# A dense SwiGLU layer with seven of eight quarter products in both halves, and expert tiles of other row counts

## The chip, the cores and the metric

The kernel runs on one core of one Trainium2 chip. The metric is the device time of one execution in microseconds. The kernel before was timed three times: median 3994.94 us, lowest 3988.59, highest 4003.63.

## The reference, cut to what matters

A trunk of two residual layers over 1024 tokens of width 1024, all in float32. The even layer ends in a dense SwiGLU with 2816 inner columns, the odd one in a mixture of eight experts with 3584 inner columns, of which each token takes two:

```python
h = h + retnet_gla_mixer(hn, positions, ...)          # ends in  o @ w_out
h = h + swiglu(rms_norm(h, norm_ffn_g[0]), w_gate, w_up, w_down)
h = h + hgrn2_mixer(hn, ...)
h = h + moe_swiglu(rms_norm(h, norm_ffn_g[1]), w_router, w_gate, w_up, w_down)
return rms_norm(h, final_norm_g)

def swiglu(h, w_gate, w_up, w_down):
    return (jax.nn.silu(h @ w_gate) * (h @ w_up)) @ w_down

def moe_swiglu(h, w_router, w_gate, w_up, w_down):
    top_logits, top_idx = lax.top_k(xt @ w_router, 2)
    ...
```

## The kernel before, in words

**Products.** Every float32 matrix is held as a high and a low part (`whi`, `wlo`; `xhi`, `xlo`), and a block product is three TensorE matmuls, high by high, high by low and low by high (`mm3`, L153). The parts are made on two engines: ScalarE copies the high part, VectorE subtracts it to get the low one (`split_to`, L819; `split`, L136). A block has 128 stationary columns; the moving side has 512 columns in the dense layer and as many as the expert tile has rows in the experts. PSUM has two rings of four banks, `pj` and `dn`.

**Order of the work.** The program is traced in order, and a list scheduler then fixes each engine's own order; an engine runs its list strictly from the front. All loads go through SyncE's queue (SP), the stores through GpSimd's (POOL). Work that may come later is handed to `defer` (L102), which runs it some ticks on; a tick is one step of the loop under way.

**Projection, L750 to L790.** Eight token tiles of 128 rows; each is 48 matmuls of 512 columns, then the residual add (L766). One tick later `done` stores the row tile, takes its norm (L188) and `place` turns it: eight TensorE transposes into PSUM, evacuated as high and low parts (L198). The halves `x[0]`, `x[1]` of turned rows are the input of the dense layer.

**Dense layer, first product, L813 to L932.** Tokens and input columns are cut in two, so the input has four quarters; gate and up columns stand as the two halves of the other side. Seven products of sums of quarters replace the eight quarter products. `quad_sums` (L823) makes the three sums from the already turned halves: add high and low (L836), combine (L841), split again (L820, L821). `quad_weights` (L866) does the like for the weights of each of 22 column blocks; each block then runs seven products of 12 matmuls, and stores its hidden tile of 128 x 1024 to scratch.

**Dense layer, second product, `ffn_down`, L934 to L980.** A plain product: token tiles in groups of 3, 3 and 2 (L42), for each group 22 inner blocks, for each block 2 column halves by each tile by 3 matmuls of 512. Each group reads the hidden rows from scratch and the whole of `ffn_w_down`. Ahead of the first hidden tile the queue carries the gain of the next norm and three row tiles `h` (L935 to L955).

**Experts, L1237 to L1388.** Eight stages in an order of load: the first is the expert with the fewest picks among the first 768 tokens, the others follow by falling count. Stage n computes a tile of `CAPS[n]` rows (L31). Gate and up are 1344 matmuls with `CAPS[n]` moving columns. Down has two forms (L1324): up to two cuts of 128 rows it is 336 matmuls of 512 columns; with three cuts of 96 it is 672 matmuls of `CAPS[n]` columns and transposes back. When an expert has more picks than its stage's rows, a branch after the eight stages runs a further whole tile of 288 rows for it and adds up all rows anew (L1258, L1481).

Of the kernel before, what the change touches and what calls it, by code (L numbers as in the profile page):

```python
# [9 lines left out]
F32 = mybir.dt.float32  # L10
F32R = mybir.dt.float32r
# [19 lines left out]
CAPS = (256, 288, 284, 280, 272, 264, 256, 256)  # L31
# [10 lines left out]
FFN_TILES = ((0, 3), (3, 3), (6, 2))  # L42
# [33 lines left out]
class Trunk:  # L76
# [136 lines left out]
    def gain_rows(self, pool, tag, ap):  # L213
        g = self.t(pool, [P, D], tag)
        self.nc.sync.dma_start(g, self.bcast_rows(ap, D))
        return g


    def build(self, upto=9):
        nc, tc = self.nc, self.tc  # L220
        with ExitStack() as ctx:
# [8 lines left out]
            with self.pool("hnp") as self.hnp:  # L230
# [3 lines left out]
                with self.pool("op") as self.op, self.pool("w2") as w2:  # L234
                    x = self.outproj_ab(oT, (w2, 0, 4))
                if upto < 2:
                    return
                pc = self.ffn(x)
# [511 lines left out]
    def outproj(self, w, src, oT, w2, pairs, done):  # L750
# [8 lines left out]
        for t in range(8):  # L759
            h = self.t(self.op, [P, D], "h", 6)  # L760
# [11 lines left out]
    def outproj_ab(self, oT, w2):  # L772

        nc = self.nc
        g = self.gain_rows(self.op, "gain", self.i["norm_ffn_g"][0])
        x = [None, None]

        def place(hn, t):
            if t % 4 == 0:
                x[t // 4] = self.half()  # L780
            self.rows_to_fm(self.dn, hn, x[t // 4], t % 4)

        def done(h, t):
            nc.gpsimd.dma_start(self.s["h0"][t * P:(t + 1) * P, :], h)
            hn = self.norm_rows(self.op, "hn", h, g)

            self.defer(max(1, 4 * (t // 4) + 3 - t), place, hn, t)

        self.outproj(self.i["ab_w_out"][0], self.i["x"][0], oT, w2, (0, 2, 3, 1), done)
        self.flush()  # L790
        return x
# [21 lines left out]
    def ffn(self, x):  # L813

        with self.pool("ffs") as fs:
            self.gate_up_quads(fs, x)
        return self.ffn_down(x)

    def split_to(self, hi, lo, src):  # L819
        self.nc.scalar.activation(hi, src, AF.Copy)  # L820
        self.nc.vector.tensor_tensor(lo, src, hi.bitcast(F32), op=OP.subtract)  # L821

    def quad_sums(self, fs, x):  # L823


        tt = self.nc.vector.tensor_tensor
        quarter = [[[a[:, 4 * c:4 * c + 4, :] for a in x[r]] for c in range(2)] for r in range(2)]

        def tiles():
            return [self.t(fs, [P, 2, HT], "raw", 8) for _ in range(2)]  # L830

        def whole(q):
            out = tiles()
            for n, o in enumerate(out):
                hi, lo = (a[:, 2 * n:2 * n + 2, :].bitcast(F32) for a in q)
                tt(o, hi, lo, op=OP.add)  # L836
            return out

        def sums(dst, a, b, op):
            for o, p, q in zip(dst, a, b):  # L840
                tt(o, p, q, op=op)  # L841
            return dst

        def split(src, name):
            s = [self.t(fs, [P, 4, HT], name + n, 1, F32R) for n in ("hi", "lo")]
            for n, r in enumerate(src):
                self.split_to(*(a[:, 2 * n:2 * n + 2, :] for a in s), r)
            return s

        a21, a22 = whole(quarter[1][0]), whole(quarter[1][1])  # L850
        s1 = sums(a22, a21, a22, OP.add)
        o1 = split(s1, "s1")
        a11 = whole(quarter[0][0])
        s2 = sums(s1, s1, a11, OP.subtract)
        o2 = split(s2, "s2")
        s3 = sums(a21, a11, a21, OP.subtract)
        a12 = whole(quarter[0][1])
        s4 = sums(a12, a12, s2, OP.subtract)

        o4 = quarter[1][0]  # L860
        for n, r in enumerate(s4):
            self.split_to(*(a[:, 2 * n:2 * n + 2, :] for a in o4), r)
        o3 = split(s3, "s3")
        return [quarter[0][0], quarter[0][1], o4, quarter[1][1], o1, o2, o3]

    def quad_weights(self, fs, w, v, c):  # L866

        nc = self.nc
        g, u = (self.t(fs, [P, 2, 4, P], "raw", 8) for _ in range(2))
# [3 lines left out]
        ta, tb = (self.t(fs, [P, 2, 4, P], "raw", 8) for _ in range(2))  # L873
        tt, wp = nc.vector.tensor_tensor, self.wps[0][0]
# [23 lines left out]
    def gate_up_quads(self, fs, x):  # L898
# [3 lines left out]
        wg, wu = (i[k][0] for k in ("ffn_w_gate", "ffn_w_up"))  # L902
        tt, act = nc.vector.tensor_tensor, nc.scalar.activation
        X = None
        for f in range(D_FF // P):
            W = self.quad_weights(fs, wg, wu, f * P)
            X = X or self.quad_sums(fs, x)
            A, B = self.pj([P, HT]), self.dn([P, HT])
            C, Dk = self.pj([P, HT]), self.dn([P, HT])
            p1, d, p5, u2 = (self.t(fs, [P, HT], "sn", 8) for _ in range(4))  # L910
            self.quad_product(A, W[0], X[0], True)
            act(p1, A, AF.Copy)
            self.quad_product(B, W[1], X[1], True)
            tt(p1, p1, B, op=OP.add)
# [19 lines left out]
    def ffn_down(self, x):  # L934
# [4 lines left out]
        with self.pool("ffn") as fp:  # L939
# [8 lines left out]
            for t0, nt in FFN_TILES:  # L948
# [21 lines left out]
                if t0 + nt == 8:  # L970
                    pc = self.piece(i["c_w_in"][0], 2048)
# [604 lines left out]
```

## Time and profile before

| what | value |
|---|---|
| median of three runs | 3994.94 us |
| the profiled execution's own time | 4001.33 us |
| its span, first to last instruction | 3999.7 us |
| TensorE busy | 3890.8 us, 97% of the span |
| VectorE, ScalarE, GpSimd busy | 51%, 38%, 7% |
| mean granted TensorE clock | 0.985 of full |

A row of stretches reads: the stretch in us from the span's start, its length, then busy us and count of instructions of PE (TensorE matmul), PEld (weight load), DVE (VectorE), ACT (ScalarE) and POOL (GpSimd), the granted clock, the share of the DMA engines, GB/s. A row of groups reads: line, engine, operation, output from input, shapes, count, busy us, mean ns of one, idle time before them and what ended it. A row of the timeline reads: start, length (from the first start to the last end of a merged run), engine, line, what, count, and in brackets the idle time before it. Matmuls are pipelined, so the length of one says less than the distance between starts.

### The profile page before, as it was taken

The page shows a single profiled execution, that of the slowest core. Times are in us where ns is not written, and L with a number is a line of the kernel's source. Part 1 is how long each engine was busy: PE and PEld are TensorE (multiplying, and loading weights), DVE is VectorE, ACT ScalarE, POOL GpSimd, SP SyncE. Part 2 cuts the span into 40 slices and gives each one's busy share as a digit, 9 for nine tenths or more (in the row PEclk, how much of TensorE's full clock was granted, in tenths as well). Part 3 has the DMA queues.
Part 4 walks back from the last instruction along what each step waited for, and adds up shares of the span by engine and source line. Part 5 has one row for each costly group of instructions (what it writes and reads, how often), then busy time and mean ns, then how long its engine had stood idle before and what let it go on. Part 6 is the DMA issues. An engine that isn't in the chain of part 4 may idle for free. (4 is left out here: it accounts for less than half of the span.)

```text
span 3999.7 us, 63991 instructions
## 1 busy us (share of the span) xinstructions
PE 3890.8 (97%) x26112; PEld 3600.7 (90%) x26112; DVE 2042.7 (51%) x3011; ACT 1500.2 (38%) x2311; POOL 279.9 (7%) x421
## 2 busy tenths in 40 slices
PE   8999989999899999999899999999999999999998
PEld 7888868888688889997798999999999999999996
DVE  5743356554355364354654544545545445455564
ACT  4212323333334222222344444434434444444443
POOL 1011000000001000003100000000000000000012
PEclk9999989999999999999899999999999999999999
DMA  4011313221665111113566555555555555556686
GB/s 133 27 48 61 127 51 99 82 82 64 193 199 184 43 33 53 43 64 123 169 194 196 168 172 172 171 161 187 185 174 177 179 185 186 189 186 199 216 285 220
DMA packets 436287, 568.17 MB, mean 142 GB/s; under 512 B 25462, under 2 KB 340118, under 8 KB 435984
## 3 DMA queue, kind: packets, MB, share of 16 engines
q1 hardware_dynamic: 414848, 493.87, 38.7%
q0 software_dynamic: 21136, 70.13, 5.0%
q8 instruction: 206, 3.38, 0.4%
q14 instruction: 97, 0.79, 0.1%
HBM read 511.11 MB, written 51.87 MB: 141 GB/s over the span
## 5 line engine op out<-in xcount | busy, mean ns | idle before, releaser
L144 DVE TENSOR_TENSOR wlo<-wst,whi 128x1024 fp32r<-128x1024 f32 (+1 forms) x816 | 995.8, 1223 | 1279.5 <-ACT whi L143 1263.8
L143 ACT ACTIVATE whi<-wst 128x1024 fp32r<-128x1024 f32 (+1 forms) x816 | 859.5, 1056 | 1092.1 <-PE pj L156 583.9
L156 PE MATMUL pj<-mxl,whi 128*128 128x256 f32 (+5 forms) x3584 | 1029.1, 287 | 0.0
L155 PE MATMUL pj<-mxh,whi 128*128 128x256 f32 (+5 forms) x3584 | 1027.6, 287 | 1.0 <-ACT sl L1316 0.6
L157 PE MATMUL pj<-mxh,wlo 128*128 128x256 f32 (+5 forms) x3584 | 1028.5, 287 | 0.0
L155 PEld LDWEIGHTS pj<-mxh,whi 128*128 128x128 f32 x3584 | 675.9, 189 | 1.8 <-ACT sl L1316 0.8
L156 PEld LDWEIGHTS pj<-mxl,whi 128*128 128x128 f32 x3584 | 675.6, 189 | 0.3 <-DVE mxl L1299 0.2
L157 PEld LDWEIGHTS pj<-mxh,wlo 128*128 128x128 f32 x3584 | 673.7, 188 | 0.0
L155 PE MATMUL pj<-whi,xhi 128*128 128x256 f32 (+2 forms) x1280 | 400.8, 314 | 5.0 <-DVE h L976 4.0
L156 PE MATMUL pj<-wlo,xhi 128*128 128x256 f32 (+2 forms) x1280 | 399.2, 312 | 0.9 <-DVE wlo L144 0.9
L157 PE MATMUL pj<-whi,xlo 128*128 128x256 f32 (+2 forms) x1280 | 399.1, 312 | 0.0
L155 PE MATMUL dn<-mhh,whi 128*128 128x288 f32 (+4 forms) x1120 | 326.3, 291 | 0.0
L157 PE MATMUL dn<-mhh,wlo 128*128 128x288 f32 (+4 forms) x1120 | 325.6, 291 | 0.0
L156 PE MATMUL dn<-mhl,whi 128*128 128x288 f32 (+4 forms) x1120 | 325.2, 290 | 0.0
L155 PEld LDWEIGHTS pj<-whi,xhi 128*128 128x128 f32 x1280 | 248.8, 195 | 17.9 <-issue 4.7
L156 PEld LDWEIGHTS pj<-wlo,xhi 128*128 128x128 f32 x1280 | 249.0, 195 | 11.5 <-DVE wlo L144 2.1
L157 PEld LDWEIGHTS pj<-whi,xlo 128*128 128x128 f32 x1280 | 248.7, 194 | 9.1
L155 PE MATMUL pj<-xhi,whi 128*128 128x512 f32 x624 | 246.1, 394 | 5.3 <-ACT whi L820 3.4
L157 PE MATMUL pj<-xhi,wlo 128*128 128x512 f32 x624 | 245.4, 393 | 0.1
L156 PE MATMUL pj<-xlo,whi 128*128 128x512 f32 x624 | 244.8, 392 | 0.0
L156 PEld LDWEIGHTS dn<-mhl,whi 128*128 128x128 f32 x1120 | 210.9, 188 | 0.0
L155 PEld LDWEIGHTS dn<-mhh,whi 128*128 128x128 f32 x1120 | 210.6, 188 | 0.0
(373 smaller groups left out, 5459.7 us busy)
## 6 DMA issues: line engine op xcount, KB each, us to landing
wst<-in_moe_w_gate_dram SPq DMA_DIRECT2D x224, 512.0 KB
wst<-in_moe_w_up_dram SPq DMA_DIRECT2D x224, 512.0 KB
wst<-in_moe_w_down_dram SPq DMA_DIRECT2D x224, 512.0 KB
wst<-in_ffn_w_down_dram SPq DMA_DIRECT2D x66, 512.0 KB
wst<-in_c_w_in_dram SPq DMA_DIRECT2D x32, 512.0 KB
wst<-in_ab_w_in_dram SPq DMA_DIRECT2D x26, 512.0 KB
scr_h<-h POOLq DMA_DIRECT2D x24, 512.0 KB, 3.5
raw<-in_ffn_w_gate_dram SPq DMA_DIRECT2D x22, 512.0 KB
```

Source lines behind the costliest of these rows:

```text
L143: act = nc.scalar.activation(hi, st, AF.Copy)
L144: dve = nc.vector.tensor_tensor(lo, st, hi.bitcast(F32), op=OP.subtract)
L155: mm(ps, l[0], r[0], start=start, stop=False, **kw)
L156: mm(ps, l[0], r[1], start=False, stop=False, **kw)
L157: self.last_mm = mm(ps, l[1], r[0], start=False, stop=stop, **kw)
```

## The change

`CAPS` becomes (224, 284, 280, 276, 270, 256, 248, 256). `quad_sums` goes; the sums of quarters are made from row tiles while the projection runs, in `done`, and turned. The second product is also done as seven products of sums of quarters, each 11 inner blocks by 4 token tiles by 3 matmuls of 512. For this the first product takes its column blocks in pairs (j and j + 11), makes the hidden sums on VectorE and the weight sums of `ffn_w_down` on GpSimd, and stores both to scratch with `keep`, eleven stores to a pair. `ffn_down` reads one stored left and one right block pair (512 KB each) per step; the rows `h` and the gain are loaded at the third tick.

```diff
-CAPS = (256, 288, 284, 280, 272, 264, 256, 256)
+CAPS = (224, 284, 280, 276, 270, 256, 248, 256)
...
+    def turn(self, rows, dst, t):
+        ps = self.dn([P, 4, P])
+        for k in range(4):
+            self.nc.tensor.transpose(ps[:, k, :], rows[:, k * P:(k + 1) * P], self.ident)
+        self.split_to(*(a[:, :, t * P:(t + 1) * P] for a in dst), ps)
...
+        def place2(hn, t, ht, s1):
+            self.turn(hn[:, R], q[1][1], t)
+            self.turn(s1, X[0], t)
+            self.turn(ht[:, L], X[1], t)
+            self.turn(ht[:, R], q[1][0], t)
         def done(h, t):
             nc.gpsimd.dma_start(self.s["h0"][t * P:(t + 1) * P, :], h)
             hn = self.norm_rows(self.op, "hn", h, g)
+            if t < 4:
+                nc.gpsimd.dma_start(self.s["hn0"][t * P:(t + 1) * P, :], hn)
+                self.defer(1, place, hn, t)
+                return
+            ht = self.t(self.op, [P, D], "ht", 1)
+            r = slice((t - 4) * P, (t - 3) * P)
+            nc.sync.dma_start(ht, self.s["hn0"][r, :])
+            s1 = h[:, L]
+            tt = (nc.vector if t > 5 else nc.gpsimd).tensor_tensor
+            tt(s1, hn[:, L], hn[:, R], op=OP.add)
+            tt(hn[:, L], ht[:, L], hn[:, L], op=OP.subtract)
+            tt(ht[:, L], s1, ht[:, L], op=OP.subtract)
+            tt(ht[:, R], ht[:, R], ht[:, L], op=OP.subtract)
+            nc.gpsimd.dma_start(self.s["s3r"][r, :], hn[:, L])
+            self.defer(1, place2, hn, t - 4, ht, s1)
+        self.outproj(self.i["ab_w_out"][0], self.i["x"][0], oT, w2, (0, 2, 3, 1), done, 3)
...
+            sn = lambda: self.t(fs, [P, HT], "sn", 10)
+            for f in [a * NH + j for j in range(NH) for a in range(2)]:
...
+                if f == 0:
+                    for t in range(4):
+                        r = sn()
+                        nc.sync.dma_start(r, self.s["s3r"][t * P:(t + 1) * P, :])
+                        self.turn(r, X[6], t)
...
+                if f < NH:
+                    a11, a21 = p1, d
+                    b = self.t(fs, [P, 2, 2, HT], "wd", 1)
+                    nc.sync.dma_start(b, wd.rearrange("(r p) (c n) -> p r c n", p=P, c=2)[:, j::NH])
+                else:
+                    a12, a22 = p1, d
...
+                    tt(s1, a21, a22, op=OP.add)
+                    self.keep("hid", 4, j, s1)
...
+                    tt(a11, s1, a11, op=OP.subtract)
+                    self.keep("hid", 5, j, a11)
...
+                    pt(b[:, 0, 0], b[:, 0, 1], b[:, 0, 0], op=OP.subtract)
...
+                    for n, a in enumerate((b[:, 0, 0], b[:, 1, 1], b[:, 0, 1], b[:, 1, 0])):
+                        self.keep("wt", n, j, a)
...
     def ffn_down(self, x):
+            def product(n, ps, first=True, last=True):
+                for j0 in range(0, NH, 2):
...
+                    own = n or j0 > 2
+                    for dst, src, pool in ((l, hv[n], fp if own else None), (r, W[n], None)):
+                        wp = self.wps[0][0]
+                        st = self.t(pool or wp, [P, 2, HT], "wst", 4 if pool else 2)[:, :nj]
+                        nc.sync.dma_start(st, src[:, js])
+                        dst += [self.t(pool or wp, [P, 2, HT], a, 3 if pool else 4, F32R)[:, :nj] for a in ("whi", "wlo")]
+                        self.split_to(*dst, st)
+                    for j in range(nj):
+                        for u in range(4):
+                            self.mm3(ps[u], [a[:, j, u * P:(u + 1) * P] for a in l], [a[:, j, :] for a in r],
                                     first and j0 + j == 0, j0 + j == NH - 1, **kw)
+                    self.tick()
+            A = [self.pj([P, HT]) for _ in range(4)]
+            self.defer(3, rows)
+            product(0, A)
+            add(0, 0, A)
+            B = [self.dn([P, HT]) for _ in range(4)]
+            product(1, B)
+            add(0, 0, B)
+            product(5, A, False)
...
+            A = [self.pj([P, HT]) for _ in range(4)]
+            product(3, A)
+            pc = self.piece(i["c_w_in"][0], 2048)
+            self.flush()
+            add(1, 0, A, OP.subtract)
+            for t in range(4, 8):
+                finish(t)
```

Here `rows` loads the eight tiles `h` and the gain; `add` adds four PSUM banks to a quarter of the rows; `finish` stores a row tile, takes its norm and turns it for the next layer. The ring `h` of the projection has three buffers where it had six; the ring `raw` of the first product has four where it had eight, and the weight sums take the ring `wst`.

## Rows read from the trace of the kernel before

**Rows 1.** The page: the span, and the first engine's busy time.

```profile
span 3999.7 us, 63991 instructions
PE 3890.8 (97%) x26112; PEld 3600.7 (90%) x26112; DVE 2042.7 (51%) x3011; ACT 1500.2 (38%) x2311; POOL 279.9 (7%) x421
```

**Rows 2.** Stretches of the dense layer.

```profile
555.30:613.30 58.00, 41.18 (x148) 29.68 (x147) 50.37 (x56) 24.49 (x34) 2.50 (x5) 0.79 0.26 80
613.30:1006.60 393.30, 393.20 (x1735) 325.25 (x1733) 217.29 (x288) 150.84 (x208) 22.16 (x41) 1.00 0.25 80
1006.60:1021.60 15.00, 0.00 (x0) 0.00 (x0) 2.97 (x4) 2.12 (x3) 0.54 (x1) 0.64 0.94 324
1021.60:1028.60 7.00, 6.92 (x17) 5.20 (x18) 1.92 (x2) 0.86 (x2) 0.00 (x0) 0.55 0.81 249
1028.60:1270.90 242.30, 241.93 (x1088) 199.57 (x1086) 123.75 (x124) 99.75 (x118) 13.18 (x18) 1.00 0.61 194
1270.90:1274.90 4.00, 0.00 (x0) 0.03 (x1) 1.97 (x3) 1.49 (x2) 0.00 (x0) 0.85 0.47 141
```

**Rows 3.** Stretches of four expert stages, from first to next first matmul.

```profile
1947.20:2188.40 241.20, 240.92 (x1708) 225.57 (x1707) 134.64 (x232) 111.67 (x151) 5.35 (x5) 1.00 0.59 185
2188.40:2459.40 271.00, 270.98 (x2053) 270.69 (x2052) 128.75 (x150) 115.09 (x154) 6.25 (x8) 1.00 0.53 172
...
3251.20:3500.40 249.20, 249.20 (x2058) 249.20 (x2057) 127.14 (x149) 113.06 (x154) 5.22 (x8) 1.00 0.58 187
3500.40:3740.60 240.20, 240.20 (x1711) 225.47 (x1710) 126.64 (x156) 111.86 (x151) 6.73 (x9) 1.00 0.61 196
```

**Rows 4.** Stretches inside gate and up, at 288 and at 256 rows.

```profile
2200.00:2350.00 150.00, 150.00 (x1133) 150.00 (x1132) 76.65 (x96) 67.67 (x95) 3.50 (x3) 1.00 0.54 170
...
3510.00:3650.00 140.00, 140.00 (x1186) 140.00 (x1185) 75.94 (x96) 67.63 (x100) 5.57 (x7) 1.00 0.62 196
```

**Rows 5.** Timeline of TensorE: matmuls of 128 moving columns, back to back.

```profile
457.38 0.39 PE L450 MATMUL dn<-vg,A 128*128 128x128 f32 x2
457.60 0.39 PE L452 MATMUL dn<-s,qq 128*128 128x128 f32 x2
457.82 0.39 PE L450 MATMUL dn<-vg,A 128*128 128x128 f32 x2
```

**Rows 6.** Groups of VectorE between projection and first product, 555.3 to 613.3 us.

```profile
L836 DVE TENSOR_TENSOR raw<-xhi,xlo 128x1024 f32<-128x1024 f32 x8 | 9.6, 1218 | 0.0
L841 DVE TENSOR_TENSOR raw<-raw,raw 128x1024 f32<-128x1024 f32 x8 | 9.4, 1219 | 0.0
...
L208 DVE SCALAR_TENSOR_TENSOR xlo<-dn,xhi 128x512 fp32r<-128x512 f32 x8 | 5.1, 685 | 1.2 <-ACT xhi L207 1.2
```

**Rows 7.** Timeline of TensorE: the last row tile turned, then the first product.

```profile
561.28 1.94 PE L205 MATMUL dn<-ident,hn 128*128 128x128 f32 x8 [2.84 <-DVE hn L195]
566.18 0.80 PE L155 MATMUL pj<-xhi,whi 128*128 128x512 f32 x1 [2.96 <-ACT whi L820]
```

**Rows 8.** Timeline of TensorE: eight transposes inside the second product.

```profile
1122.73 1.03 PE L205 MATMUL dn<-ident,hn 128*128 128x128 f32 x8
1123.52 0.47 PE L155 MATMUL pj<-whi,hh 128*128 128x512 f32 x1
```

**Rows 9.** Groups of GpSimd, whole span: stores, adds of 512 columns.

```profile
L925 POOL DMA_DIRECT2D scr_hid<-sn x22 | 12.0, 544 | 349.1 <-DVE sn L924 349.1
...
L624 POOL TENSOR_TENSOR qk<-qk,t 128x512 f32<-128x512 f32 x8 | 10.2, 1278 | 31.2 <-DVE t L623 30.9
```

**Rows 10.** Timeline of SP's queue ahead of the second product.

```profile
1009.41 0.38 SPq L215 DMA_DIRECT2D gain<-in_norm_mix_g_dram  x1
1009.85 1.41 SPq L954 DMA_DIRECT2D h<-scr_h  x3
1011.36 1.96 SPq L959 DMA_DIRECT2D hid<-scr_hid  x3
```

**Rows 11.** Timeline of TensorE where the second product starts.

```profile
1006.12 0.39 PE L157 MATMUL pj<-s3hi,wlo 128*128 128x512 f32 x1
1021.67 0.80 PE L155 MATMUL pj<-whi,hh 128*128 128x512 f32 x1 [15.17 <-ACT hh L820]
```

**Rows 12.** Groups of VectorE in the first product: an add of 512 columns.

```profile
L924 DVE TENSOR_TENSOR sn<-sn,sn 128x512 f32<-128x512 f32 x21 | 14.5, 692 | 0.7
```

More of the change, by code (lines that the diff above doesn't have):

```diff
@@ L233, in build @@
                     oT = self.mix_ab(x)
[L234 to L238, printed above, removed]
+                x = [None, None]
+                with self.pool("fs") as fs:
+                    X = [[self.t(fs, [P, 4, HT], f"s{n}{a}", 1, F32R) for a in ("hi", "lo")] for n in range(2)]
+                    with self.pool("op") as self.op, self.pool("w2") as w2:
+                        self.outproj_ab(oT, (w2, 0, 4), X)
+                    if upto < 2:
+                        return
+                    q = [[[a[:, 4 * c:4 * c + 4, :] for a in oT[r]] for c in range(2)] for r in range(2)]
+                    self.ffn_gate_up([q[0][0], q[0][1], q[1][0], q[1][1], X[0], X[1], None])
+                pc = self.ffn_down(x)
                 if upto < 3:
@@ L747, in mix_c, with outproj @@
         return oT
-    def outproj(self, w, src, oT, w2, pairs, done):
+    def outproj(self, w, src, oT, w2, pairs, done, nh=6):
         nc = self.nc
@@ L810, in outproj_c @@
         self.route_end()
[L813 to L864, printed above, removed]
     def quad_weights(self, fs, w, v, c):
         nc = self.nc
-        g, u = (self.t(fs, [P, 2, 4, P], "raw", 8) for _ in range(2))
+        wp = self.wps[0][0]
+        g, u = (self.t(fs, [P, 2, 4, P], "raw", 4) for _ in range(2))
         for t, a in ((g, w), (u, v)):
@@ L872, in quad_weights @@
                               a.rearrange("(k p) c -> p k c", p=P)[:, :, c:c + P])
[L873 to L874 removed]
+        ta, tb = (self.t(wp, [P, 2, 4, P], "wst", 2) for _ in range(2))
+        tt = nc.vector.tensor_tensor
         def split(src):
@@ L939, in ffn_down, with rows, finish @@
         with self.pool("ffn") as fp:
-            g = self.gain_rows(fp, "gain", i["norm_mix_g"][1])
-            def finish(h, t):
+            g = self.t(fp, [P, D], "gain")
+            hs = [self.t(fp, [P, D], "h", 8) for _ in range(8)]
+            def rows():
+                for t, h in enumerate(hs):
+                    nc.sync.dma_start(h, self.s["h0"][t * P:(t + 1) * P, :])
+                self.gain_rows_to(g, i["norm_mix_g"][1])
+            def finish(t):
+                nc.gpsimd.dma_start(self.s["h1"][t * P:(t + 1) * P, :], hs[t])
@@ new lines, in add @@
+            def add(r, c, ps, op=OP.add):
+                for u in range(4):
+                    hc = hs[4 * r + u][:, c * HT:(c + 1) * HT]
+                    tt(hc, hc, ps[u], op=op)
+            A = [self.pj([P, HT]) for _ in range(4)]
[6 more added lines that the diff above has]
+            product(5, A, False)
+            add(0, 1, A)
+            B = [self.dn([P, HT]) for _ in range(4)]
@@ L979, in ffn_down @@
+            product(4, B)
+            add(1, 1, B)
+            product(6, A, False)
+            add(1, 0, A)
+            add(1, 1, A)
+            product(2, B, False)
+            add(0, 1, B)
+            for t in range(4):
+                self.defer(1 + t, finish, t)
+            A = [self.pj([P, HT]) for _ in range(4)]
+            product(3, A)
+            pc = self.piece(i["c_w_in"][0], 2048)
             self.flush()
+            add(1, 0, A, OP.subtract)
+            for t in range(4, 8):
+                finish(t)
```

148 lines of the change are left out of this document (71 added, 77 removed).

## The prediction

> **What bounds the kernel now.** I read the page first: TensorE is busy 97% of the span [rows 1], so an edit pays if it takes TensorE work away or closes one of its few gaps. Then I read the stretches of the dense layer [rows 2]. The reader is to see a calm first product (393.3 us, clock 1.00, no idle time) between two troubled places: 58.0 us at the start of the layer, where TensorE works 41.2 and VectorE 50.4, and 15.0 us ahead of the second product, where TensorE does nothing and the DMA engines are at 0.94. The stretches of the experts [rows 3] have no idle time at all; there only the number and the width of matmuls count. The price of a dense matmul is a distance between starts, not a length: 393.3 us / 1735 = 0.227 us for 512 columns [rows 2].
>
> The sum below stands against the profiled execution's own 4001.3 us (span 3999.7 [rows 1]); that is 6.4 us above the median of 3994.9, so I take 6.4 off at the end. A measurement of this kernel can tell about 0.5%, 20 us, from no change.
>
> **Expert tiles.** Three cuts: between 288 and 264 rows a stage falls from 271.0 to 249.2 us [rows 3], 0.91 us per row. Stages 2 to 5 lose 4, 4, 4 and 2 rows: 14 x 0.91 = 12.7 us. Stage 6 goes from 264 to 256 and thereby into the two-cut form, which a stage of 256 rows has now: 249.2 - 240.2 = 9.0 us [rows 3]. Stage 7, 256 to 248, keeps the two-cut form, whose down product streams 512 columns whatever the tile; only gate and up shrink. A gate or up matmul takes 150 us / 1133 = 132.4 ns at 288 and 140 / 1186 = 118.0 ns at 256 rows [rows 4], 0.45 ns a row; 8 x 0.45 x 1344 = 4.8 us. Stage 1, 256 to 224, is off the measured widths. On the line it would save 32 x 0.45 x 1344 = 19.4 us. But matmuls of only 128 moving columns start 0.22 us apart in pairs, 0.11 each [rows 5], where the line would give 60 ns: something besides the moving columns holds them, and 224 on the line (103.6 ns) would be below that. Ends: 0 and 19.4 us; I take the floor of the row, 112 ns, the nearest measured: (118.0 - 112) x 1344 = 8.1 us. Sum of the stages: 12.7 + 9.0 + 4.8 + 8.1 = 34.6 us less.
>
> The Trainium skill, "TensorE: Matmul & The Clock Gate", section LDWEIGHTS, names what could hold them: the load of the stationary operand goes by that operand's columns, P / 1.2 ns, so a narrower tile doesn't shorten it. Its 106.7 ns for 128 columns would make stage 1 an estimated 15.2 us shorter instead of 8.1; the row says 112, and whether the float32 pairs of that row and the expert matmuls load alike no row tells.
>
> **Second product.** 22 x 8 x 2 x 3 = 1056 matmuls become 7 x 11 x 4 x 3 = 924, all of 512 columns: 132 x 0.227 = 29.9 us less. The transposes of the next layer's rows stay 64. The new partial adds (36 of 512 columns where 16 were, 0.69 us each [rows 12]) lie on VectorE beside products of 30 us each; a product that writes the same four banks again starts one whole product later. Their cover is gone only at the end, where the four last adds release the banks for the next layer: now 4.0 us [rows 2], and again the same chain, so 0 (from -3 to +4).
>
> **Start of the layer.** The 58.0 us hold 148 TensorE instructions: 32 transposes and 116 matmuls, 116 x 0.227 = 26.3 us; so 31.7 us go beyond products. The chain now: the last row tile is turned after waiting for its norm, then the weights come [rows 7], and VectorE makes the sums (9.6 + 9.4 us, and eight splits of 1.2 [rows 6]). The sums from turned halves go. New are, per late row tile, four adds of 512 columns (0.69 on VectorE [rows 12]; 1.28 on GpSimd [rows 9] for two tiles) and 16 transposes where there were 8. Eight cost about 0.9 us of TensorE, from their start to the first undelayed matmul [rows 8]. Behind the last projection matmul stand 32 of them as now (3.6 us), 16 more for the third sum inside the first block (1.8), and 32 more than now stand earlier, within the projection: +3.6 us. What else is left: VectorE has an add, a norm (1.3), four sums, eight evacuations of 0.69 and the first block's weight work (four adds, 3.5 splits of 1.2) to do, some 17 us in all; TensorE meanwhile has the transposes and the first two products of 12, whose quarters were ready long before, 9 us. I take 5 us of wait, 2 for the last evacuation of the third sum, and 1.3 for matmuls at the low clock level, since a wait as long as now leaves the clock at 0.79 [rows 2]. Left are 3.6 + 1.8 + 5 + 2 + 1.3 = 13.7; 31.7 - 13.7 = 18 us less. Ends: 24 if nothing waits, 6 if the weights again land only when the row buffers are free, as at 566.18 [rows 7]. `done` now also puts a load of 512 KB and a store on SP and POOL; the load of `ht` has one buffer and waits for the turn before it, inside the 5 us. The three `h` buffers of the projection bring the next load a tile earlier than the add needs it: 0.
>
> **First product.** Its matmuls are the same. VectorE gets four adds a pair of blocks, 2.8 us on 38, with 55% busy now [rows 2, 12]; GpSimd gets eleven stores and four subtractions, 11 x 0.54 + 4 x 1.28 = 11.1 us on 38 [rows 9]. Nothing there ends last: 0, unless the stores come late (a rival, below).
>
> **Hand-over to the second product.** Now: 15.0 us without work plus 17 matmuls in 7.0 us at clock 0.55, 3.1 us too many [rows 2]; 18 us. Hidden rows wait in SP's queue behind the gain and three row tiles [rows 10], and TensorE for them [rows 11]. After: the first two steps use buffers outside the new pool, so their loads run under the last block and TensorE goes on at once for 48 matmuls, 10.9 us. Then comes what is late next: step three needs space that the last stores release, and the eight row tiles and the gain, 4.7 MB, pass through the same queue around it, 14.6 us at the 324 GB/s that the DMA engines reached there [rows 2]. Issued at +1 us they hold step three to about +21 instead of +10.9; issued behind it, they hold step four. I take 10 us of wait and 3 at the low clock; 18 - 13 = 5 us less. Ends: 18 less (the order puts them where there is room), 8 more.
>
> **The sum:** 34.6 + 29.9 + 18 - 3.6 + 5 = 83.9 us. 4001.3 - 83.9 = 3917.4, less 6.4: **3911 us**. By the page's weight load alone it would be 3904.
>
> **The rivals.**
> - *The narrow tile goes down the line.* Nothing holds 224 columns, stage 1 saves 19.4: 3911 - 11 = 3900 us. For it: the line is straight from 288 to 256 [rows 4]. Against: the 112 ns [rows 5]. 0.12.
> - *The second product becomes bound by its loads.* It reads two blocks of 512 KB per 24 matmuls (5.4 us), 40.4 MB over the seven products, with the rows 49 MB. At today's 194 GB/s that is 254 us for 210 us of matmuls: 3955 us. Against: today's rate is what is asked, at 0.61 of the engines; 324 GB/s at 0.94 were reached [rows 2]. 0.06.
> - *The stores hold the first product.* A pair of blocks takes nine buffers of a ring of ten, so the next pair's second tile waits until the store of `a11` has landed. If the subtractions and weight stores stand ahead of it in GpSimd's queue, it lands some 7 us later, ScalarE waits for it with everything behind, and TensorE loses about 6 us a pair: 66 us, 3977 us, no change that can be told. From about 10 us a pair the whole would be slower. 0.06.
> - *Slower: an expert overflows.* The reference's own routing, evaluated on its inputs, gives the stages 208, 283, 280, 276, 269, 256, 248 and 228 picks against 224, 284, 280, 276, 270, 256, 248 and 256 rows. Four stages are full to the last row. One pick more in one of them and the branch behind the eight stages runs a further tile of 288 rows, 271.0 us [rows 3], and adds all rows up again: 4182 us or more. The place is the comparison in `rank`; it decides at one token. Against: the closest second and third logit of any token are 0.0065 apart with logits of spread 7.9, far above what three matmuls of split parts leave out. 0.03.
>
> **How the numbers follow.** The forecast has 0.70; 0.03 is left for mishaps of either kind. The low end takes the good ends together in part: experts 11 more, start 6, hand-over 7, 3911 - 24 = 3887; with the other good ends about 3878. The high end: start 12 worse, hand-over 12, experts 8, tail 4, about 3947, which nearly takes in the bound loads. Range 3878 to 3948. Faster by over 0.5% (below 3975) hold the forecast, the first two rivals and most mishaps: 0.90. Within 0.5%: the stores, 0.05. Slower: overflow, or the stores at their worst, 0.05.
>
> **What would show it.** Right: stage 1 about 233 us and stage 6 about 240; 924 dense matmuls in the second product at 0.227 us; the start of the layer near 40 us to the same matmul; TensorE running on past the first product and stopping once, some 11 us in, for a split. Wrong: a distance of 104 or of 118 ns at 224 columns; one wait at every pair of blocks behind a store; waits at every step of the second product behind a load; a ninth expert stage.

## The result, and the profile after

| | us |
|---|---|
| before, median of 4 runs | 3999.28 (3988.59 to 4003.83) |
| after, median of 4 runs | 3939.18 (3933.18 to 3942.27) |
| ratio, 95% interval | 0.9852 (0.9826 to 0.9878) |
| forecast | 3911 (3878 to 3948) |
| profiled execution after: time, span | 3942.27, 3940.5 |

The change is faster by 1.5%, inside the range and 28 us above the forecast. The spans differ by 59.2 us where the sum said 83.9. First the page after, which answers to [rows 1]:

```profile
span 3940.5 us, 63330 instructions
PE 3825.2 (97%) x25660; PEld 3520.1 (89%) x25660; DVE 2064.4 (52%) x3046; ACT 1477.6 (37%) x2292; POOL 398.0 (10%) x555
```

TensorE is busy 97% as before, but 65.6 us less. The stretches of the dense layer after, for [rows 2] (start of the layer, rest of the first product, then the second product in three parts):

```profile
560.50:612.20 51.70, 41.61 (x177) 32.40 (x176) 39.65 (x60) 21.37 (x32) 20.98 (x23) 0.83 0.77 243
612.20:1019.30 407.10, 395.23 (x1722) 325.37 (x1722) 250.94 (x320) 146.81 (x205) 106.48 (x142) 0.99 0.43 141
1019.30:1034.70 15.40, 10.98 (x49) 8.76 (x47) 9.35 (x12) 5.62 (x6) 2.71 (x5) 1.00 0.87 308
1034.70:1054.70 20.00, 14.36 (x44) 10.71 (x45) 6.15 (x7) 4.22 (x6) 0.00 (x0) 0.74 1.00 366
1054.70:1247.00 192.30, 192.30 (x866) 159.62 (x865) 108.30 (x116) 79.05 (x92) 9.06 (x13) 1.00 0.58 192
```

The second row is the surprise: 1722 matmuls at 0.22665 us are 390.3 us, and the stretch takes 407.1, where before it had no idle time. TensorE is idle for 11.9 us of it, and busy 4.9 us longer than these matmuls need, at a granted clock of 0.99. Next the stretches after of the mixer behind the layer, of expert stages one, two, six, seven and eight, for [rows 3], and of what lies behind the last matmul; under them the mixer, stage eight and the end before:

```profile
1247.00:1913.00 666.00, 638.76 (x4355) 574.58 (x4353) 324.78 (x749) 166.99 (x372) 80.50 (x130) 0.98 0.23 72
...
1913.00:2152.40 239.40, 235.75 (x1708) 215.53 (x1708) 133.38 (x232) 109.67 (x150) 4.88 (x5) 0.98 0.58 186
2152.40:2421.90 269.50, 269.45 (x2054) 269.22 (x2053) 128.33 (x150) 114.67 (x154) 6.01 (x8) 1.00 0.54 173
...
3201.90:3442.00 240.10, 240.10 (x1710) 225.41 (x1709) 125.48 (x145) 111.88 (x151) 5.35 (x7) 1.00 0.60 193
3442.00:3679.50 237.50, 234.99 (x1698) 218.54 (x1697) 125.58 (x155) 110.52 (x149) 6.15 (x8) 1.00 0.61 198
3679.50:3916.50 237.00, 237.00 (x1681) 222.06 (x1679) 146.82 (x164) 110.27 (x157) 40.59 (x52) 1.00 0.79 264
3916.50:3940.50 24.00, 0.37 (x2) 0.00 (x0) 2.66 (x4) 2.86 (x6) 4.51 (x8) 0.57 0.11 41
```

```profile
1274.90:1947.20 672.30, 645.72 (x4338) 582.60 (x4338) 321.14 (x744) 164.55 (x365) 77.69 (x125) 0.96 0.22 71
...
3740.60:3982.60 242.00, 238.57 (x1680) 221.88 (x1679) 146.54 (x164) 110.00 (x157) 40.71 (x52) 1.00 0.77 259
3982.60:3999.70 17.10, 0.41 (x2) 0.00 (x0) 2.71 (x4) 2.86 (x6) 4.51 (x8) 0.64 0.15 58
```

From these rows the account of the 59.2 us:

| part | predicted | seen |
|---|---|---|
| projection's end, 555.3 to 560.5 | +3.6 | +5.2 |
| start of the layer, beyond products: 31.7 to 22.9 | -18 | -8.8 |
| rest of the first product | 0 | +16.8 |
| hand-over: 18.1 to 14.8 (35.4 less 91 x 0.2266) | -5 | -3.3 |
| second product, 132 matmuls fewer at 0.22665 us | -29.9 | -29.9 |
| its tail, 4.0 to nothing | 0 | -4.0 |
| 16 of its transposes moved into the mixer, and what is left over | 0 | -3.9 |
| mixer, 672.3 to 666.0 | 0 | -6.3 |
| eight expert stages, 2035.4 to 2003.5 | -34.6 | -31.9 |
| behind the last matmul, 17.1 to 24.0 | 0 | +6.9 |

Two of these rows belong to this pair of executions and not to the change. The mixer's 6.3 us are the clock's (see the two halves below). And 5.0 of the 31.9 us of the experts are stage eight, whose tile stays at 256 rows: over the fourteen traces kept here, from its first to its last matmul, it took 237.0 to 242.3 us.

**Where the first product waits.** Timeline of the changed kernel, by engine: SP's queue, VectorE, ScalarE, TensorE.

```profile
685.68 0.76 SPq L858 DMA_DIRECT2D raw<-in_ffn_w_gate_dram  x1
703.58 0.37 SPq L928 DMA_DIRECT2D wd<-in_ffn_w_down_dram  x1
704.04 0.42 SPq L858 DMA_DIRECT2D raw<-in_ffn_w_up_dram  x1
...
710.59 1.43 DVE L870 TENSOR_TENSOR wst<-raw,raw 128x512 f32<-128x512 f32 x1 [13.26 <-DMA raw<-in_ffn_w_up_dram]
...
717.55 0.63 ACT L921 ACTIVATE sn<-sn 128x512 f32<-128x512 f32 x1 [14.77 <-DVE sn L920]
...
675.94 0.50 PE L154 MATMUL pj<-xhi,whi 128*128 128x512 f32 x1 [2.79 <-ACT sn L908]
718.72 0.80 PE L154 MATMUL pj<-s1hi,whi 128*128 128x512 f32 x1 [5.51 <-ACT sn L901]
```

SP issues no load for 17 us, then `wd` and at once the up weights behind it. `wd` has one buffer and waits until the four sums of the pair before are stored; the up weights wait in the same queue. VectorE stands 13.26 us at the weight sum, its gate result (L920) behind it; ScalarE waits for that 14.77 us with an evacuation behind, and TensorE 5.51 us for the evacuation. That reading is the theory which the runs had to test. The waits of SP's queue from 612 to 1020 us (waited for, us in total, times, longest) and the eleven issues of `wd` (durations in ns, first and last start in us) go with it:

```profile
SPq L928 <- DMA scr_wt<-wd: 110.3, 15, 16.1
```

```profile
L928 SPq DMA_DIRECT2D wd<-in_ffn_w_down_dram x11: 367/368/2856, 564.2 to 734.3; - x11
```

In SP's order all eleven `wd` loads stand within the first 170 us, far ahead of the pairs that they belong to. TensorE's four waits (2.8, 5.5, 0.7 and 2.8 us) come in the later part of these loads, between 676 and 747 us; after that, with no `wd` load left to issue, it has none.

### The profile page after: what moved, and what is told of

The parts are those of the page before. It is cut to its first block, busy times and chain, and to the rows that moved or that the text cites. A ratio compares the mean times of both kernels' runs of the same rounds, so it can differ in the third digit from the quotient of the medians.

```text
span 3940.5 us, 63330 instructions
## 1 busy us (share of the span) xinstructions
PE 3825.2 (97%) x25660; PEld 3520.1 (89%) x25660; DVE 2064.4 (52%) x3046; ACT 1477.6 (37%) x2292; POOL 398.0 (10%) x555
## 3 DMA queue, kind: packets, MB, share of 16 engines
q0 software_dynamic: 28032, 92.96, 6.7%
## 4 chain that ended last, share of the span: by engine, by line
PE 76%; DMA 3%; DVE 3%; POOL 1%; ACT 1%; issue 1%; SPq 0%; POOLq 0%; DVEq 0%; ACTq 0%
PE pj L154 17%; PE pj L155 17%; PE pj L156 17%; PE dn L154 7%; PE dn L155 7%; PE dn L156 7%; PE dn L391 2%; DMA wd<-in_ffn_w_down_dram 1%; DVE wlo L143 0%; DMA scr_wt<-wd 0%; PE dn L437 0%; PE pj L1351 0%; ACT whi L142 0%; PE dn L1094 0%; DMA wst<-in_moe_w_down_dram 0%
## 5 line engine op out<-in xcount | busy, mean ns | idle before, releaser
L143 DVE TENSOR_TENSOR wlo<-wst,whi 128x1024 fp32r<-128x1024 f32 (+1 forms) x750 | 914.7, 1222 | 1180.0 <-ACT whi L142 1167.0
L142 ACT ACTIVATE whi<-wst 128x1024 fp32r<-128x1024 f32 (+1 forms) x750 | 789.9, 1056 | 1000.0 <-PE pj L155 556.7
L154 PE MATMUL pj<-mxh,whi 128*128 128x256 f32 (+6 forms) x3584 | 1020.3, 285 | 2.2 <-DVE sl L1372 2.2
L156 PE MATMUL pj<-mxh,wlo 128*128 128x256 f32 (+6 forms) x3584 | 1021.1, 285 | 0.0
L155 PE MATMUL pj<-mxl,whi 128*128 128x256 f32 (+6 forms) x3584 | 1021.0, 285 | 0.0
L154 PE MATMUL dn<-mhh,whi 128*128 128x284 f32 (+3 forms) x896 | 261.4, 292 | 0.0
L156 PE MATMUL dn<-mhh,wlo 128*128 128x284 f32 (+3 forms) x896 | 260.4, 291 | 0.0
L155 PE MATMUL dn<-mhl,whi 128*128 128x284 f32 (+3 forms) x896 | 260.3, 291 | 0.0
L782 DVE TENSOR_TENSOR wlo<-wst,whi 128x1024 fp32r<-128x1024 f32 (+1 forms) x128 | 149.9, 1190 | 142.9 <-ACT whi L781 131.6
L781 ACT ACTIVATE whi<-wst 128x1024 fp32r<-128x1024 f32 (+1 forms) x128 | 126.2, 1009 | 223.0 <-PE pj L155 123.6
```

The costliest lines, as they stand in the source:

```text
L142: act = nc.scalar.activation(hi, st, AF.Copy)
L143: dve = nc.vector.tensor_tensor(lo, st, hi.bitcast(F32), op=OP.subtract)
L154: mm(ps, l[0], r[0], start=start, stop=False, **kw)
L155: mm(ps, l[0], r[1], start=False, stop=False, **kw)
L156: self.last_mm = mm(ps, l[1], r[0], start=False, stop=stop, **kw)
```

## The experiments

**The two halves alone.** Edits: the new CAPS in the kernel before, and the old CAPS in the changed one.

```diff
-CAPS = (256, 288, 284, 280, 272, 264, 256, 256)
+CAPS = (224, 284, 280, 276, 270, 256, 248, 256)
```

> Only the expert tiles are cut; the dense layer is that of the kernel before. By the prediction's terms 34.6 us less than before (ratio 0.9914). By the stages of the changed kernel's trace about 25 us less (0.9938), of which some 7 us are lost again after the last stage, so the eight stages by themselves should give about 32. If the longer end of the changed kernel (24.0 us behind the last stage where there were 17.1) comes from the dense layer's additional stores, it is 17 us here; if it comes from the expert tiles or varies from run to run, it isn't.

> Only the dense layer is changed; the expert tiles are those of before. By the prediction's terms 49.3 us less than before (ratio 0.9877). By the changed kernel's trace: projection +5, first product with its start +8, second product with its hand-over -41, that is 28 us less, and 34 with the 6 us by which the next mixer was shorter (0.9915 to 0.993). If the mixer's 6 us came by chance (its clock was 0.97 to 0.99 in four stretches before), the mixer is as long as before in some of the runs here.

Measured: expert tiles alone 3970.24 us, ratio 0.9937 (0.9921 to 0.9953); dense layer alone 3974.88, ratio 0.9940 (0.9921 to 0.9958); before 3997.26. The prediction's ratios, 0.9914 and 0.9877, both lie outside these intervals; the dense layer is the half that missed by more, 22 us against 49. The two halves together give 49 us where the whole change gives 60; with intervals of this width that difference isn't shown to be more than noise. The stretches behind the last matmul, tiles alone and dense layer alone:

```profile
3943.00:3959.63 16.63, 0.37 (x2) 0.00 (x0) 2.66 (x4) 2.86 (x6) 4.51 (x8) 0.58 0.16 60
```

```profile
3949.00:3973.10 24.10, 0.34 (x2) 0.00 (x0) 2.63 (x4) 2.86 (x6) 4.52 (x8) 0.57 0.11 41
```

So the longer end comes with the dense layer. The mixer took 667 and 668 us here by the same measure (last dense matmul to first expert matmul) by which it took 677 before and 666 after. With the kernel before's own dense layer it is 667, at a granted clock of 1.00 from 1300 to 1900 us: the mixer's 6.3 us belong to one execution, not to the change.

**The early loads of `wd`.** Edit: the load moves to the second block of a pair, and is not issued before that block's last weight load (`self.raw`).

```diff
             W = self.quad_weights(fs, wg, wu, f * P)
+            if f >= NH:
+                b = self.t(fs, [P, 2, 2, HT], "wd", 1)
+                with self.tc.issue_after(self.raw.ins):
+                    nc.sync.dma_start(b, wd...[:, f - NH::NH])
...
-                b = self.t(fs, [P, 2, 2, HT], "wd", 1)
-                nc.sync.dma_start(b, wd...[:, j::NH])
```

> As the changed kernel, but the block of the down weights from which the sums are made is loaded in the second block of each pair, and not before the last gate and up loads of that block have been issued. Theory: the early loads of it wait in SP's queue for a free buffer, and the next block's gate and up loads stand behind them. Then the waits of TensorE in the first product (17 us of it beyond 0.227 us a matmul, 676 to 747 us after the start) go, and the weight sums of the first block are no longer slowed by GpSimd's subtractions beside them (0.69 instead of 1.8 us each, some 4 us): 15 to 20 us less than the changed kernel, about 3920. Rival one: the loss comes from the ring of ten result tiles waiting for stores; then the waits stay and the time is that of the changed kernel, 3939. Rival two: what is lost is the four-buffer ring of the gate and up loads, with the same result.

Measured: 3923.66 us, ratio 0.9817 (0.9802 to 0.9833), 15.5 below the changed kernel. Its SP queue and its stretch for the rest of the first product:

```profile
697.48 0.37 SPq L858 DMA_DIRECT2D raw<-in_ffn_w_up_dram  x1
702.99 0.37 SPq L858 DMA_DIRECT2D raw<-in_ffn_w_gate_dram  x1
716.54 0.37 SPq L858 DMA_DIRECT2D raw<-in_ffn_w_up_dram  x1
717.12 0.41 SPq L900 DMA_DIRECT2D wd<-in_ffn_w_down_dram  x1
```

```profile
L900 SPq DMA_DIRECT2D wd<-in_ffn_w_down_dram x11: 371/407/574, 573.6 to 945.6; - x11
```

```profile
609.50:999.50 390.00, 390.00 (x1723) 322.92 (x1722) 250.82 (x320) 148.35 (x205) 115.73 (x151) 1.00 0.45 154
```

The eleven loads are now spread to 945.6 us, and no idle time is left, with the same ten result tiles, the same four weight buffers and the same GpSimd work: the queue was the cause, and both rivals fall.

The second half of the expectation is about VectorE's weight sums beside GpSimd's. Timelines of the changed kernel, VectorE and GpSimd, and below of the paced one:

```profile
574.73 1.76 DVE L870 TENSOR_TENSOR wst<-raw,raw 128x512 f32<-128x512 f32 x1
...
573.64 2.30 POOL L945 TENSOR_TENSOR wd<-wd 128x512 f32<-128x512 f32 x1 [4.86 <-DMA wd<-in_ffn_w_down_dram]
```

```profile
574.81 0.68 DVE L870 TENSOR_TENSOR wst<-raw,raw 128x512 f32<-128x512 f32 x1
...
584.78 1.78 DVE L870 TENSOR_TENSOR wst<-raw,raw 128x512 f32<-128x512 f32 x1
```

The slow sums move with GpSimd's work. Of the 88 weight sums of the changed kernel ten took 1.43 to 1.92 us, each beside a subtraction on GpSimd; the others took 0.68. Where VectorE does the subtractions itself (the last but one run below) none of the 88 took more than 0.69. The Trainium skill, "SBUF — State Buffer", section "Who interferes with whom", says that a VectorE instruction with both inputs in SBUF contends with a GpSimd instruction that reads SBUF; these rows agree. From the last projection matmul to the 127th matmul of the product it is 48.9 us with the paced load, 47.9 to 51.7 in four further versions with it, and 50.3 to 53.0 in six without: on average some 2.5 us of the start, though the two ranges overlap.

**The hand-over.** In the changed kernel TensorE runs on past the first product and then waits twice:

```profile
1034.76 0.50 PE L154 MATMUL pj<-whi,whi 128*128 128x512 f32 x1 [4.49 <-ACT whi L781]
1047.65 0.80 PE L154 MATMUL pj<-whi,whi 128*128 128x512 f32 x1 [5.54 <-ACT whi L781]
```

Edit: eight row loads in two halves, the first later.

```diff
-            self.defer(3, rows)
...
+            self.defer(4, half, 0)
+            self.defer(16, half, 1)
```

> As the changed kernel, but the row tiles of the second product and the gain are loaded in two halves, the first at its fourth step (the add needs it after the sixth), the second at the sixteenth, in place of all at the third. Theory: step three is late because 4.7 MB of rows and its own loads share the DMA engines; then the two waits of TensorE there (4.5 and 5.5 us, with 2.7 at the low clock) shrink to 5 us or less together, and the whole is 5 to 10 us shorter than the changed kernel, about 3932. Rival: step three is late because its buffers only come free with the last stores of the first product, whatever stands beside it; then the first wait stays (4 to 5 us) and at most the second goes, some 3 us.

Measured: 3935.89 us, ratio 0.9852 (0.9836 to 0.9868). In the time of the whole this can't be told from the changed kernel; in the trace the second product is 7.6 us shorter (220.1 for 227.7). One wait is left:

```profile
1037.19 0.79 PE L154 MATMUL pj<-whi,whi 128*128 128x512 f32 x1 [4.98 <-ACT whi L781]
```

Both theories got half: the rows caused the second wait, and the first is not theirs.

**The narrow expert tile.** Edits of the changed kernel, one in each run:

```diff
-CAPS = (224, 284, 280, 276, 270, 256, 248, 256)
+CAPS = (208, 284, 280, 276, 270, 256, 248, 256)
...
+CAPS = (256, 284, 280, 276, 270, 256, 248, 256)
```

> As the changed kernel, but the first expert's tile has 208 rows, the number of its picks. If a floor of 112 ns lies under a gate or up matmul, whatever its columns, the 1344 of the first stage stay at 112 ns, and the stage at the length that it has with 224 rows (236 to 239 us in four kernels). If the moving columns go on counting, at 0.45 ns a row, they start 105 ns apart and the stage is 9.7 us shorter. The time of the whole: 3939 by the first, 3930 by the second.

> As the changed kernel, but the first expert's tile has 256 rows, as before. By the distances of 118.2 and 111.8 ns the 1344 gate and up matmuls of stage one take 8.6 us longer, and so should the stage (246 to 248 us). The rival: stage one is held by its loads, which are no fewer with a narrower tile, and the 224 rows gained only part of it: then it is 241 to 242 us here, as in the two kernels that have 256 rows, and the narrower tile was worth 3 to 5 us.

Single runs, 3947.53 and 3944.03 us; the stages tell more. Stage one was 236.7 us with 208 rows and 241.2 with 256. Timeline of TensorE with 224 rows, and with 208:

```profile
1994.83 0.27 PE L156 MATMUL pj<-mxh,wlo 128*128 128x224 f32 x1
1995.16 0.28 PE L156 MATMUL pj<-mxh,wlo 128*128 128x224 f32 x1
```

```profile
1994.91 0.27 PE L156 MATMUL pj<-mxh,wlo 128*128 128x208 f32 x1
1995.24 0.27 PE L156 MATMUL pj<-mxh,wlo 128*128 128x208 f32 x1
```

Three starts in 0.33 us in both: 112 ns was the median in either stage. The floor of the prediction holds, below 224 columns nothing more is gained. But gate and up took 156.2 us with 224 rows where 1344 x 111.8 ns are 150.3, and 160.7 with 256 (before). Of the 5.9 us beyond, 3.3 lie at the start of the stage: its first 34 matmuls took 7.1 us at a granted clock of 0.53, where at 112 ns they are 3.8; with 256 rows (before) this cost 1.2. The waits of TensorE in stage one of the changed kernel (waited for, us in total, times, longest):

```profile
PE pj L154 <- DVE sl L1372: 2.2, 2, 1.2
PE pj L1351 <- DVE sl L1372: 1.5, 2, 0.9
```

The first two, 2.2 us, lie in gate and up, the other two just behind. `sl` stands on VectorE behind splits of weight blocks that had only just landed; the chain of waits goes through the gate weights for 6.54 us at 1958.08. In ten kernels with 224 rows the stage took 234.2 to 239.4 us, in three with 256 rows 241.2 to 242.0: the tile is worth about 4 us, as the rival had it. That the loads hold the stage is read from the chain; no run gave them more room.

**The end.** Edit: the stores of the weight sums from ScalarE's queue.

```diff
-        self.nc.gpsimd.dma_start(self.s[name][r:r + P, :], a)
+        (self.nc.scalar if name == "wt" else self.nc.gpsimd).dma_start(...)
```

> As the changed kernel, but the 44 stores of the weight sums are issued from ScalarE's queue in place of GpSimd's. For the end of the kernel: behind the last output GpSimd drains, 4.4 us before, 4.2 and 10.0 us with the expert tiles alone and the dense layer alone, 9.8 us in the changed kernel. If that length goes by the number of transfers that GpSimd issued (205 before, 287 after, 243 here), it is about 6.9 us here and the semaphore update before it about 1.9 (1.26 before, 2.58 after); if it is something else of the dense layer, both stay at 9.8 and 2.6. The first product may become longer, since ScalarE then waits at a store for GpSimd's subtraction; that is no part of the question.

A single run of 3959.67 us, with waits of 7.3, 6.6 and 7.1 us in the first product behind ScalarE, as feared. GpSimd's drain took 5.87 us, the semaphore update 1.62: both shorter, and below the 6.9 and 1.9 that the count of transfers gave. The stretch behind the last matmul:

```profile
3938.40:3957.64 19.24, 0.43 (x2) 0.00 (x0) 2.72 (x4) 2.86 (x6) 4.51 (x8) 0.59 0.13 52
```

**The norm first.** Edit, with a second `ht` and three normed tiles:

```diff
-            self.defer(1, place2, hn, t - 4, ht, s1)
+            self.defer(2 if t == 6 else 1, place2, hn, t - 4, ht, s1)
```

> As the changed kernel, but the turning of the next to last row tile is put behind the norm of the last one, with a second ht buffer and three in place of four normed tiles. Theory: at the start of the layer TensorE waits 4.2 us for the last tile's norm, since its square stands on ScalarE behind four evacuations of 0.48 us each; then the wait is about 2 us shorter and the layer's start too (the same matmul, 612.2 us after the start, comes at about 610). Rival: the evacuations only move behind the norm and are waited for there, the work of ScalarE and VectorE being the bound; then the start is as long as it was, within 0.5 us.

A single run of 3938.80 us. Timelines of TensorE, the changed kernel and this one:

```profile
566.50 1.08 PE L788 MATMUL dn<-ident,hn 128*128 128x128 f32 x4 [4.20 <-DVE rank L1255]
569.64 1.08 PE L788 MATMUL dn<-ident,ht 128*128 128x128 f32 x4 [1.20 <-issue]
573.60 0.80 PE L154 MATMUL pj<-xhi,whi 128*128 128x512 f32 x1 [1.63 <-ACT whi L781]
```

```profile
564.20 1.09 PE L788 MATMUL dn<-ident,hm 128*128 128x128 f32 x4 [2.74 <-DVE hm L194]
566.64 1.09 PE L788 MATMUL dn<-ident,h 128*128 128x128 f32 x4 [1.35 <-issue]
569.04 1.08 PE L788 MATMUL dn<-ident,ht 128*128 128x128 f32 x4 [1.31 <-issue]
573.00 0.80 PE L154 MATMUL pj<-xhi,whi 128*128 128x512 f32 x1 [1.63 <-ACT whi L781]
```

The wait shrinks by 1.5 us and returns behind it, most of it at the next tile (1.35 us): ahead of the first matmul it is 7.2 us in all, as before the edit. From the last projection matmul to the first of the product it is 13.7 us for 13.4: the start is as long as it was, as the rival had it; that ScalarE and VectorE together bound this place is its reading, and no run shows it by itself. (To the 127th matmul it was 50.0 us here, against the 50.3 to 53.0 above, so that total shows nothing.)

**Together.** The paced loads, the split rows, and a third step in the buffers outside the pool; then this with one store of the four weight sums.

```diff
-                    own = n or j0 > 2
+                    own = n or j0 > 4
```

```diff
...
-                    for n, a in enumerate((b[:, 0, 0], b[:, 1, 1], b[:, 0, 1], b[:, 1, 0])):
-                        self.keep("wt", n, j, a)
+                    nc.gpsimd.dma_start(self.s["wt"].rearrange("(r c f p) n -> p r c f n", r=2, c=2, p=P)[:, :, :, j], b)
```

> The paced load of the down weights and the split row loads together, and the third step of the second product's first product loads its hidden rows into the buffers outside the new pool as well. Theory: the wait of 5.0 us that stayed with the split rows is a wait for space which the last stores of the first product release, so it goes with the buffers outside the pool; the first product is as without gaps as with the paced load alone. Sum against the changed kernel: 16 for the paced load, 4 to 8 for the rows, 5 for the third step, that is 25 to 29 us less, about 3911 to 3914. Rival: the third step needs its weights' and its hidden rows' transfers, which start only when the second step's buffers are free, so the wait moves but stays 3 to 5 us; then 19 to 24 us less, about 3916 to 3920.

> As the one with the third step, but the four weight sums of a pair are stored by one transfer of 1 MB in place of four of 256 KB: the bytes are the same, GpSimd issues 33 transfers fewer (254 in place of 287). If the drain at the end goes by the number of transfers, it is 7.6 us and the time 2 to 3 us shorter than with four stores; if it goes by bytes, it stays at 9.8 us and the time is the same.

Measured: 3911.82 us, ratio 0.9792 (0.9778 to 0.9806), and 3914.12, ratio 0.9794 (0.9780 to 0.9807). With the third step's version the second product took 215.4 us where the changed kernel took 227.7, and this is the only wait left in it:

```profile
1021.89 1.20 PE L154 MATMUL pj<-whi,whi 128*128 128x512 f32 x4 [1.33 <-ACT whi L781]
```

The first wait was one for buffer space: it is 5.06 us with the paced load alone and 4.98 with the split rows alone, and goes where the third step has buffers of its own as well. (Paced load and split rows together without these buffers were not run.) One store in place of four left the drain at 9.71 us and the time where it was: the number of transfers doesn't set it.

Last, on the third step's version, the weight sums on VectorE with their stores on ScalarE's queue, and the stores alone on SP's:

```diff
-        tt, act, pt = nc.vector.tensor_tensor, nc.scalar.activation, nc.gpsimd.tensor_tensor
+        tt, act, pt = nc.vector.tensor_tensor, nc.scalar.activation, nc.vector.tensor_tensor
...
-        self.nc.gpsimd.dma_start(self.s[name][r:r + P, :], a)
+        (self.nc.scalar if name == "wt" else self.nc.gpsimd).dma_start(...)
```

```diff
-        self.nc.gpsimd.dma_start(self.s[name][r:r + P, :], a)
+        (self.nc.sync if name == "wt" else self.nc.gpsimd).dma_start(...)
```

> As the one with the third step, but the weight sums are made on VectorE in place of GpSimd, and their 44 stores issued from ScalarE's queue. The drain at the end goes with the packets of GpSimd's queue (21136 packets 4.40 us, 24512 packets 5.87, 28032 packets 9.79): here some 22500 and thus 5 to 6 us, with the semaphore update 5 us less in all. VectorE gets 4 x 0.69 us a pair of blocks more and the first product should still have no wait over 1 us behind its first 50 us: then about 3907. Rival: ScalarE, which has the evacuations of every product in its queue, waits there for VectorE's sums ahead of each store, as the waits of about 7 us did where its queue had the stores of GpSimd's sums; then the first product is 10 us or more longer and the gain at the end is gone.

> As the one with the third step, but the 44 stores of the weight sums are issued from SP's queue, among the loads. The end is 5 us shorter, as with ScalarE's queue. Theory of the held queue: a store in SP's queue waits for GpSimd's sums with the next block's gate and up loads behind it; whether TensorE then waits goes by how far ahead of their use these loads are. If they have more than the some 8 us that the four sums take, the first product stays as it is (about 3907); if not, it gets a wait of several us a pair in part of its eleven pairs, and is 10 us or more longer.

Measured: 3911.47 us, ratio 0.9791 (0.9775 to 0.9806), and 3909.01, ratio 0.9779 (0.9762 to 0.9796). The end was 18.8 and 19.0 us for 24.4, and in both the rest of the first product took 390.1 us, without a wait of TensorE over 0.2 us. So the paced order leaves room for the stores in either queue, and the rivals fall. In the profiled executions the mixer took 673.8 and 673.2 us, with three falls of the granted clock in each, against 664.9 without one with the third step (last section): 9 us by the clock alone, which hides the 5.4 us in the time of single runs. That either version beats the third step isn't shown; all four beat the changed kernel.

## Why the prediction was right, and where it was off

**The direction and most of the size** came from counting matmuls, and there the terms held: 132 x 0.22665 = 29.9 us in the second product, stage six -9.1 for -9.0, stages two to five -13.3 for -12.7, a distance of 112 ns at 224 columns, and TensorE running on past the first product before it stopped.

**Luck** helped: without the clock in the mixer (6.3 us) and the shorter stage eight (5.0 us), neither of which the change made, this pair of executions would stand 48 us apart and not 59. The experts' -31.9 looks near to -34.6 only by stage eight; the stages that were cut gave 26.9.

**First product.** The step that failed is "Nothing there ends last: 0". I added up busy time on VectorE and GpSimd, and left out the eleven `wd` loads of 1 MB on SP's queue. They have one buffer, freed by GpSimd's last store, and in SP's order they ran far ahead, with the next weights behind them: +16.8 us, and the paced loads gave back all of it. The rival of the late stores had the releaser right (stores behind GpSimd's sums), but put the wait at the ring of result tiles, at every pair and 66 us; it came through a load's buffer, four times in all, at a quarter of that.

**Start of the layer, -8.8 for -18.** The mechanism was right, two terms were too small. The sum had 7 us of waits, "5 us of wait" and 2 for the third sum; seen are 10.1: 4.2, 1.2, 0.2 and 1.6 ahead of the first matmul, and 1.3, 0.5 and 1.1 behind it. And it had 1.3 us for the low clock: of the 22.9 us beyond products 7.4 are neither waits nor the 5.4 of the transposes, at a granted clock of 0.83 over the stretch. That was the larger miss. For the waits I had counted VectorE alone; the norm goes through ScalarE, GpSimd and VectorE in turn, and four weight sums took 4.4 us longer beside GpSimd.

**Hand-over, -3.3 for -5.** Size right (10.0 us of wait for 10, and 4.8 for 3 at the low clock), cause half right: of the two waits only the second came from the rows in the queue; the first was for space, as the prediction also named.

**Stage one, -1.8 for -8.1,** about -4 over all kernels. Floor right; the cover failed: with faster matmuls the weight blocks are late, and the start at the low clock cost 2.1 us more than before. Stage seven, -2.7 for -4.8, waited 2.5 us for `sl` behind gate and up. By the weight-load figure of the Trainium skill, "TensorE: Matmul & The Clock Gate", section LDWEIGHTS (106.7 ns), the matmuls would have gained more than the row's floor; the traces show 112 ns at 224 and at 208 columns, so there is a floor, 5 ns above that figure; whether the weight load sets it, no run here shows.

**Not in the sum at all:** +6.9 at the end, and -4.0 where the four last adds no longer hold TensorE, one beyond my -3. Its adds were also miscounted: 32 of 512 columns run, not 36, which moved nothing.

## What to carry to other kernels

A new load on a queue that is issued in order is priced by what stands behind it while it waits for its buffer, not by its bytes: list its releaser, and issue it behind the loads that are needed first. When an edit adds work "beside" a calm stretch, follow each engine's order once through a pair of iterations; busy shares of 55 and 30% did not show this wait. And subtract a stretch by stretch account before reading totals: falls of the clock elsewhere made 6.3 us, more than several of the terms.

## What was not expected of the hardware

**GpSimd's drain at the end grows with what its queue carried.** The trace has a drain on GpSimd behind the last output. By the packets of queue q0: 20976 packets 4.24 us (tiles alone), 21136 4.40 (before), 24512 5.87 (three kernels, the same to the nanosecond), 27504 9.71, 28016, 28032 and 28096 9.79 in each, 28192 10.04 (dense layer alone). It isn't a straight line, and 33 transfers fewer at the same bytes changed it by 0.08. Issuing the 44 stores of the weight sums elsewhere took 3.9 us off it in three runs; why it is so stays open. The rows of the queue, before and after:

```profile
q0 software_dynamic: 21136, 70.13, 5.0%
```

```profile
q0 software_dynamic: 28032, 92.96, 6.7%
```

**The granted clock fell in the mixer in some executions and not in others, behind the same short waits.** TensorE waits there three times for some 1.3 us ahead of small matmuls: 1.28, 1.28 and 1.26 us with VectorE's weight sums, 1.27, 1.26 and 1.26 with the third step. In the first run the clock then falls to its low level (0.5 of full, 1.2 GHz), and it is 129.7 us from one such wait to the next; in the second run it stays at 2.4 GHz, and it is 126.6 and 126.5 us. The stretches behind the first of the waits, in the one run and in the other:

```profile
1406.40:1413.40 7.00, 7.00 (x36) 7.00 (x35) 3.57 (x8) 0.39 (x1) 0.00 (x0) 0.51 0.00 0
```

```profile
1407.00:1414.00 7.00, 7.00 (x65) 7.00 (x64) 5.03 (x11) 0.39 (x1) 0.00 (x0) 1.00 0.01 2
```

Three such falls made the same mixer code 673.8 us where it was 664.9. What decides whether the clock falls, no run here shows.
